# Attention projections of the second layer in scaled half-precision pairs

## The chip, the cores and the metric

The kernel runs on one core of a Trainium2 chip. The metric is the device time of one execution in microseconds (us). The core has five engines that work side by side and wait for each other through semaphores: TensorE (PE, matrix products; its weight loads are a track of their own, PEld), VectorE (DVE), ScalarE (ACT), GpSimd (POOL) and SyncE (SP). SP and POOL issue most of the DMA transfers in this kernel.

## The reference

Two layers of a backbone over 1024 latent tokens with 256 context tokens, model width 1024. The first layer mixes tokens with Fourier and Hyena channels, the second with neighbourhood attention in which the latent queries also see all context keys. Each layer ends with a SwiGLU feed-forward network (FFN). All inputs are float32. Cut to what the change touches, the second layer is:

```python
u_lat = modulate(rms_norm(h_lat, norm1_g[1]), sh1, sc1)        # (1, 1024, 1024)
u_ctx = modulate(rms_norm(h_ctx, norm1_g[1]), csh1, csc1)      # (1, 256, 1024)
q, k, v = (heads(t) for t in jnp.split(u_lat @ w_qkv, 3, axis=-1))   # 16 heads of 64
kc, vc = (heads(t) for t in jnp.split(u_ctx @ w_qkv[:, D_MODEL:], 2, axis=-1))
y_lat = neighbourhood_attention(q, k, v, kc, vc, rpb).reshape(B_, L, D_MODEL) @ w_out
h_lat = h_lat + g1 * y_lat
...
h_lat = h_lat + g2 * swiglu(modulate(rms_norm(h_lat, norm2_g[1]), sh2, sc2), ...)
```

In `neighbourhood_attention` a query of the 16 x 64 grid of latent tokens sees an 8 x 16 window of latent keys with a position bias, and all 256 context keys, under one softmax with scale 1/8.

## The kernel before

**Number format.** A product of float32 matrices is made from pairs. Each operand is split into a high part and a low remainder, and three products are added in PSUM: high x high, high x low, low x high. Two kinds of pair are in use. In the *full* kind both parts have the type `F32R`, four bytes an element (`split`, lines 287 and 289). In the *half* kind both parts are `F16` (`half_split`, lines 1153 and 1154): the operand is first multiplied by a scale, a column of per-partition numbers computed on the chip, so that it fits float16, and the result is multiplied back later. The FFNs of the latent tokens use half pairs (products at line 1342 for gate and up, at 1564 for down; some last blocks stay full). Everything else that the change touches uses full pairs, and its matmuls are issued by `mm`, line 283.

A half pair needs a bound on its operand. For weights `abs_sums` (line 1187) has ACT add up absolute values of a tile along each row, and `over_partitions` adds the rows with a small matmul. For normalised activations `operand_scale` derives the bound from the modulation columns, with a maximum over partitions on POOL (line 1172).

**Tiles.** Activations are kept transposed, in 8 blocks of 128 channels; tokens are cut into two latent pieces of 512 (`pc` 0 and 1) and the context piece of 256 (`pc` 2). A weight tile is 128 x 1024 float32, 512 KB. It is loaded into `ws`, ACT writes the high part `wh`, DVE the low part `wl`; each of the three has 2 buffers. Wide working tiles of 4 KB per partition (`S4`, name `s` in the profile) have 20 buffers, tiles of 2 KB (`S2`, also `s`) have 34. PSUM has 6 buffers `ps` and 2 `pq`.

**Stages that matter here,** in order of time:

1. First output projection (`out_proj`, about 715 to 835 us): 8 output blocks for the token pieces 2 and 0, then 8 for piece 1. Per block one weight tile, 24 matmuls of 512 columns per latent piece and 24 of 256 for the context; DVE adds the result to `h` (line 1132), ACT squares it for the next norm (line 476), POOL stores it (`ldr`, line 274).
2. FFN of the context tokens, then of the latent tokens (`ffn(0, ...)`, to about 1660 us). Near the end of gate and up, `down_scales` computes the scales of the down projection. `after2` normalises each finished piece with `norm_block` into `u1`, the input of the attention layer.
3. Values (`values`, about 1660 to 1760 us): the activations are the stationary operand, the weight halves of 512 columns are the moving one; ACT copies the result (line 1702), DVE takes its maximum (line 1703), SP stores it. After that one scale for all values is computed.
4. Attention (`attention`, about 1760 to 2260 us). `attn_prep` makes, for one pair of heads at a time, keys (three pieces) and queries (two pieces) by full-pair matmuls into `pq`; `attn_item` is a quarter of a head's queries: scores, softmax on DVE and ACT, transposes, product with the values. The loop advances three items by one step each, an older one by a later step, and after each step draws matmuls of the next pair's `attn_prep` so that these fill PE while softmax runs. `attn_out` transposes the output of a pair, multiplies it by the inverse value scale, splits it and stores both parts.
5. Second output projection: `first_part(0)`, the first 6 of 8 input blocks for piece 0, is woven into the end of the attention loop; `last_part(0)`, `first_part(1)` and `last_part(1)` follow (to about 2335 us). `add_h` (line 2141) multiplies by the modulation column and adds to `h`.

**Order.** The program is written in one order and a scheduler at compile time arranges each engine's instructions, starting what is ready and giving out tile buffers as they come free; each engine and each DMA queue then works strictly in its arranged order.

Of the kernel before, what the change touches and what calls it, by code (L numbers as in the profile page):

```python
# [19 lines left out]
P = 128  # L20
# [11 lines left out]
KSTART = (0, 8, 24, 32)  # L32
PAD_C, PAD_T, SHIFT = 120, 112, 16
BOPS = ("B11", "B21", "T2", "T1", "T3", "B22", "T4")
# [167 lines left out]
class Builder:  # L202
# [60 lines left out]

    def DR(self, shape):
        return self.dr.tile(shape, F32, name=self.nm("d"), tag=self.nm("dt"))

# [83 lines left out]
    def new_act(self, pcs=PCS, wide=True, blocks=range(KB)):  # L350

        act = Act()
        for pc in (0, 1):
            for b in blocks if pc in pcs else ():
                if wide:
                    t = self.S4(F32R)
                    act.put(0, b, pc, t[:, :512])
                    act.put(1, b, pc, t[:, 512:])
                else:
                    act.put(0, b, pc, self.S2(F32R))  # L360
                    act.put(1, b, pc, self.S2(F32R))
# [7 lines left out]
        return act  # L369

    def setup(self):
# [145 lines left out]
    def norm_block(self, x, b, pc, l, m, act, r):  # L517

        nc = self.nc
        w = WID[pc]  # L520
        sh, sc = self.ada_col(l, pc, m, b), self.ada_col(l, pc, m + 1, b)
        t = self.T()
        nc.vector.scalar_tensor_tensor(t[:, :w], x[b], sc, r[:, :w], op0=MUL, op1=MUL)
        hi, lo = act.ap(0, b, pc), act.ap(1, b, pc)
        nc.scalar.activation(hi, t[:, :w], AF.Identity, bias=sh)
        nc.vector.scalar_tensor_tensor(lo, t[:, :w], sh, hi.bitcast(F32), op0=ADD, op1=SUB)

    def norm(self, h, pcs, l, m, act):
# [584 lines left out]

    def out_proj(self, wname, y, groups, h, l, m, after):
        nc, a = self.nc, self.a
# [39 lines left out]

    def operand_scale(self, l, m):

        nc = self.nc
        conds = (0, 1) if l == 0 else (0,)
        b = self.C(4)  # L1160
        v = self.C(4)
        for c in conds:
            for k in (0, 1):
# [5 lines left out]
                                           op0=MUL, op1=ADD)  # L1169
        if l == 0:  # L1170
            nc.vector.tensor_tensor(b[:, 0:1], b[:, 0:1], b[:, 1:2], MAX)
# [8 lines left out]
        self.ucol = cols  # L1180
        self.usi = us[:, 1:2]

    def abs_sums(self, tiles, st):

        junk = self.T(BF16, 1024)
        for k, t in enumerate(tiles):
            self.nc.scalar.activation(junk[:, :t.shape[1]], t, AF.Abs, scale=2.0 ** -15, accum_out=st[:, k:k + 1])

    def over_partitions(self, sums):
# [201 lines left out]
    def ffn(self, l, u, h, hs, second, after, keep=None, begun={}):  # L1391
# [75 lines left out]
        for i in range(n2):  # L1467
# [212 lines left out]
    def values(self, u):  # L1680
# [31 lines left out]
        nc.vector.tensor_scalar(self.vs, m1, 8192.0, None, op0=MUL)  # L1712
        nc.vector.tensor_scalar(self.vsi, m2, 1.0 / 8192.0, None, op0=MUL)

    def attn_prep(self, pr, u):
# [36 lines left out]
        if pr == 0:  # L1752
            self.aw = self.weights(a["wk"][0])
# [16 lines left out]
        for pc in (0, 1):  # L1770
            for i, s in enumerate(lin(*wq, pc, acc, by_chunk)):
                if i == 3:
                    value(len(vt))
                if pc == 1 and i == 3 and pr < 7:
                    nxt = self.weights(a["wk"][pr + 1])
                yield s
            for hd in (0, 1):
                own, other = slice(hd * 64, hd * 64 + 64), slice(64 - hd * 64, 128 - hd * 64)
                qh, ql = self.S2(F32R), self.S2(F32R)
                nc.scalar.mul(qh[own], acc[pc][own], 0.125)  # L1780
                nc.vector.scalar_tensor_tensor(ql[own], acc[pc][own], 0.125, qh[own].bitcast(F32), op0=MUL, op1=SUB)
                for t in (qh, ql):
# [16 lines left out]
    def attention(self, u, fill):  # L1799
        self.prep = {}  # L1800
        self.od = [[self.DR([P, LAT]) for _ in range(2)] for _ in range(8)]
        self.banks = 6
# [127 lines left out]
    def run(self):  # L1930
# [157 lines left out]
        def after1(pcs):  # L2088
            spill(h, hs0, pcs)
            if 0 in pcs:  # L2090
# [4 lines left out]
                load_h((1,))  # L2095
                self.operand_scale(0, 3)
                for _ in self.wino_first(h, 0, 3, rs[1]):
# [11 lines left out]
        def after2(pc):  # L2109
# [15 lines left out]
        for i, _ in enumerate(self.values(u1)):  # L2125
            if i < 6:
                next(self.last, None)
        h2, o, h4 = Act(), Act(), Act()

        def load_o(b, pcs, load=None):  # L2130
            for part in (0, 1):
                if 0 in pcs:
                    t = self.S4(F32R)
                    o.put(part, b, 0, t[:, :512])
                    o.put(part, b, 1, t[:, 512:])
                for pc in pcs:
                    (load or self.ldr)(o.ap(part, b, pc).bitcast(F32), self.od[b][part][:, pc * 512:pc * 512 + 512])

        def add_h(nb, pc, acc):
            t = h2.ap(0, nb, pc)  # L2140
            nc.vector.scalar_tensor_tensor(t, acc, self.ada_col(1, pc, 2, nb), t, op0=MUL, op1=ADD)  # L2141

# [30 lines left out]
        def last_part(pc):  # L2173
            for i in (0, 1):
                wh, wl = self.weights(a["w_out2"][4 * i:4 * i + 4, :, 768:].rearrange("n p k -> p n k"), 1024, True)
                for j in range(4):
# [6 lines left out]
        for i, _ in enumerate(first_part(1)):  # L2183
            if i == 2:
                c = self.rms_begin(0)
            if i == 3:
                self.operand_scale(1, 3)
            if i == 5:
# [122 lines left out]
```

## Time and profile before

| what | value |
|---|---|
| median of 3 runs | 3006.52 us (3006.5 to 3006.53) |
| the profiled execution | 2994.77 us |
| its span, first to last instruction | 2993.0 us |
| mean granted TensorE clock | 0.984 |
| PE busy | 2844.3 us, 95%, 16366 matmuls |
| PEld busy | 1951.5 us, 65% |
| DVE / ACT / POOL busy | 71% / 55% / 18% |
| DMA | 551.49 MB, mean 184 GB/s |

How to read it: `L283 PE MATMUL ps<-s,wh 128*128 128x512 f32 x700` is a group of 700 matmuls issued at line 283, written to a PSUM tile `ps` from tiles `s` and `wh`, with a 128 x 128 stationary operand and 512 columns of four-byte elements. After the bar stand busy time in us and the mean duration of one in ns, after the next bar the idle time of the engine just before them and what ended it. Durations of neighbouring matmuls overlap in the records; the spacing of their starts is what one more of them costs a stream. A row of the table by stage gives the window, its length, busy time and instruction count of each engine, the granted clock, the DMA engines' busy share and GB/s.

### The profile page before, as it was taken

The numbers are of one execution on the slowest core, as the hardware profiler recorded it, in microseconds if no ns is written. First come the engines' busy times: TensorE is split into PE (matmuls) and PEld (weight loads), VectorE is DVE, ScalarE is ACT, GpSimd is POOL, SyncE is SP. The second block draws the span as 40 slices with busy tenths as digits, with TensorE's granted clock in tenths as the row PEclk, the third lists the DMA queues.
The fourth block names the chain that finished last, engine by engine and source line by source line (L and its number), as shares of the span: only waits on it lengthen the run. The fifth ranks groups of instructions, "written<-read, shape, count | busy, mean of one in ns | idle before, by whom it ended". The sixth has DMA issues, their size and how long they took to land. (4 is left out here: it accounts for less than half of the span.)

```text
span 2993.0 us, 46520 instructions
## 1 busy us (share of the span) xinstructions
PE 2844.3 (95%) x16366; PEld 1951.5 (65%) x16366; DVE 2132.5 (71%) x4159; ACT 1648.9 (55%) x3201; POOL 530.7 (18%) x883
## 2 busy tenths in 40 slices
PE   7899999899998999999999999999998799999997
PEld 3678888888898444444558888887786344444554
DVE  5768786684577888868876447777776888676755
ACT  4663325453456666645564337777774577564543
POOL 1012013352110111221110002222231022112000
PEclk9899999999999999999999999999999899999999
DMA  7564545357565555659864344444654376424663
GB/s 258 190 195 169 170 154 174 113 185 233 177 226 191 202 197 197 227 200 335 308 229 148 125 126 125 134 130 122 203 167 173 135 263 223 154 99 173 232 197 113
DMA packets 253684, 551.49 MB, mean 184 GB/s; under 512 B 33926, under 2 KB 69448, under 8 KB 253450
## 3 DMA queue, kind: packets, MB, share of 16 engines
q1 hardware_dynamic: 191658, 357.63, 36.5%
q0 software_dynamic: 59488, 186.70, 17.8%
q10 hardware_dynamic: 2304, 4.20, 0.4%
q8 instruction: 128, 2.10, 0.3%
q14 instruction: 106, 0.87, 0.1%
HBM read 420.20 MB, written 119.80 MB: 180 GB/s over the span
## 5 line engine op out<-in xcount | busy, mean ns | idle before, releaser
L1342 PE MATMUL ps<-s,s 128*128 128x512 f16 x2340 | 526.3, 381 | 15.4 <-ACT g L1347 12.8
L1342 PEld LDWEIGHTS <-s 128*128 128x128 f16 x2640 | 258.7, 98 | 338.6 <-issue 32.7
L283 PE MATMUL ps<-s,wh 128*128 128x256 f32 (+1 forms) x1756 | 387.9, 327 | 0.8 <-ACT wh L287 0.8
L283 PEld LDWEIGHTS ps<-s,wh 128*128 128x128 f32 x1756 | 290.0, 188 | 35.3 <-ACT wh L287 2.3
L283 PE MATMUL pq<-s,wh 128*128 128x512 f32 (+1 forms) x996 | 302.8, 383 | 4.2 <-DVE s L2141 2.9
L1564 PE MATMUL ps<-s 128*128 128x512 f16 (+2 forms) x1308 | 302.9, 378 | 2.1 <-DVE s L1154 1.7
L1153 ACT ACTIVATE s<-s,c 128x512 f16<-128x512 f32 x295 | 200.5, 715 | 118.6 <-DMA s<-d 85.7
L1564 PEld LDWEIGHTS <-s 128*128 128x128 f16 x1536 | 148.5, 98 | 179.2 <-issue 6.7
L1154 DVE SCALAR_TENSOR_TENSOR s<-s,c,s 128x512 f16<-128x512 f32 x295 | 210.5, 746 | 65.7 <-ACT s L1153 64.9
L283 PE MATMUL ps<-s,wl 128*128 128x256 f32 (+1 forms) x878 | 253.7, 327 | 2.2 <-DVE wl L289 2.2
L287 ACT CAST wh<-ws 128x1024 fp32r<-128x1024 f32 (+1 forms) x99 | 100.3, 1013 | 258.0 <-PE ps L283 173.8
L283 PE MATMUL ps<-s,s 128*128 128x64 f16 (+3 forms) x2663 | 217.6, 233 | 22.5 <-DVE st L1853 9.4
L283 PEld LDWEIGHTS pq<-s,wh 128*128 128x128 f32 x996 | 179.6, 190 | 39.3 <-DVE s L2141 3.5
L289 DVE TENSOR_TENSOR wl<-ws,wh 128x1024 fp32r<-128x1024 f32 (+1 forms) x99 | 116.5, 1177 | 118.4 <-ACT wh L287 117.2
L1342 PE MATMUL ps<-s,wh 128*128 128x512 f16 x624 | 189.9, 382 | 3.0 <-ACT wh L1153 1.7
L335 ACT CAST mat<-cs 128x1024 fp32r<-128x1024 f16 (+2 forms) x120 | 111.8, 935 | 133.6 <-PE ps L283 38.5
L283 PE MATMUL pq<-s,wl 128*128 128x512 f32 (+1 forms) x498 | 184.7, 380 | 0.5 <-DVE wl L289 0.5
L283 PE MATMUL ps<-s,mat 128*128 128x512 f32 x684 | 179.2, 409 | 5.5 <-ACT s L287 2.7
L274 POOL DMA_DIRECT2D d<-s x153 | 82.6, 541 | 518.6 <-DVE s L1410 137.1
L283 PEld LDWEIGHTS ps<-s,wl 128*128 128x128 f32 x878 | 161.3, 188 | 19.6 <-DVE wl L289 3.2
L283 PEld LDWEIGHTS ps<-s,mat 128*128 128x128 f32 x684 | 131.8, 195 | 41.3 <-DVE s L289 5.6
L283 PEld LDWEIGHTS ps<-s,s 128*128 128x128 f32 (+1 forms) x743 | 112.9, 191 | 35.2 <-DVE s L614 4.2
(410 smaller groups left out, 5734.4 us busy)
## 6 DMA issues: line engine op xcount, KB each, us to landing
s<-d SPq DMA_DIRECT2D x286, 256.0 KB, 4.4
s<-in_down SPq DMA_DIRECT2D x154, 256.0 KB, 5.1
d<-s POOLq DMA_DIRECT2D x137, 256.0 KB, 2.6
d<-tk POOLq DMA_DIRECT2D x98, 256.0 KB, 4.9
s<-in_ada_w POOLq DMA_DIRECT2D x48, 512.0 KB, 4.9
g<-in_bias POOLq DMA_DIRECT2D x128, 192.0 KB, 3.2
s<-in_up SPq DMA_DIRECT2D x46, 512.0 KB, 3.6
s<-in_gate SPq DMA_DIRECT2D x44, 512.0 KB, 4.1
```

The source lines that it names most:

```text
L274: self.last_ldr = self.nc.gpsimd.dma_start(out, in_).ins
L283: self.nc.tensor.matmul(o, l, r, start=st, stop=sp)
L287: self.last_hi = nc.scalar.copy(hi, src).ins
L289: self.last_lo = eng.tensor_tensor(lo, src, hi.bitcast(F32), SUB).ins
L335: self.nc.scalar.copy(m, st)
L1153: nc.scalar.activation(hi, src, AF.Copy, scale=scale)
L1154: nc.vector.scalar_tensor_tensor(lo, src, scale, hi, op0=MUL, op1=SUB)
L1342: nc.tensor.matmul(ps, x[:, sl], y, start=first and j == 0 and x is wh and y is xh, stop=j == 3 and x is wl, skip_group_check=True)
L1564: m = nc.tensor.matmul(acc[j][:, c0:c1], x[:, sl], y[:, xs], start=first and k == 0, stop=last and k == 2, skip_group_check=True)
```

## The change

- **Weights.** A new `weights16` loads a tile as before and makes a half pair with a scale. It replaces `weights` for the tiles of `wv`, `wk`, `wq` and `w_out2`.
- **Activations.** `norm_half` writes `u1` as half pairs, from modulation columns that are multiplied by the scale; `new_half` gives two blocks of a latent piece one wide tile, where one block had one.
- **Scales.** `qkv_sums` loads all 32 tiles of the four weights on POOL's queue into wide tiles and has ACT take their absolute sums. It is a generator that is drawn on once per output block of the first output projection, two tiles each. `qkv_scales` turns the sums into four weight scales and the inverse factors, near the end of the FFN of the first layer.
- **Undoing the scales.** The inverse factors are folded into multiplications that stood there already: the queries' 0.125 becomes the column `qinv`; the inverse value scale takes up `oinv` and goes into a scaled modulation column `g2col`, used by `add_h`.
- **Attention output.** `attn_out` writes both parts into one `F16` tile and stores them in one transfer; `load_o` reads them back the same way.
- Some small column tiles are added, and a padding tile grows from 120 to 136 numbers per partition.

The diff, cut to its core:

```diff
+    def weights16(self, src, scale, w=1024, cut=False, load=None):
+        st = self.pw.tile([P, 1024], F32, tag="ws", name=self.nm("ws"))
+        hi, lo = (self.pw.tile([P, 1024], F16, tag=g, name=self.nm(g)) for g in ("wh", "wl"))
+        (load or self.ld)(st.rearrange("p (n k) -> p n k", n=4) if cut else st[:, :w], src)
+        self.half_split(st[:, :w], scale, hi[:, :w], lo[:, :w])
+        return hi, lo
...
+    def norm_half(self, x, b, pc, act, r, cols):
...
+        nc.vector.scalar_tensor_tensor(t[:, :w], x, sc, r[:, :w], op0=MUL, op1=MUL)
+        hi, lo = act.ap(0, b, pc), act.ap(1, b, pc)
+        nc.scalar.activation(hi, t[:, :w], AF.Identity, bias=sh)
+        nc.vector.scalar_tensor_tensor(lo, t[:, :w], sh, hi, op0=ADD, op1=SUB)
...
                 acc = self.lin(wh, wl, 0, range(KB), y, pcs)
+                next(fill, None)
...
+    def qkv_sums(self):
+        a = self.a
+        self.qs = self.C(32)
+        src = [a["wv"][ch, kp] for ch in range(2) for kp in range(4)]
+        src += [a[n][b] for n in ("wq", "wk", "w_out2") for b in range(KB)]
+        for k, x in enumerate(src):
+            t = self.S4()
+            self.ldr(t, x)
+            self.abs_sums([t], self.qs[:, k:k + 1])
+            if k % 2:
+                yield
...
+    def qkv_scales(self):
+        nc = self.nc
+        bounds = self.over_partitions(self.qs.rearrange("p (i k) -> p i k", k=1))
+        t = self.C(8)
+        nc.vector.tensor_reduce(t[:, :4], bounds.rearrange("p (i k) -> p i k", k=8), axis=AX, op=MAX)
...
+        self.u1col, usi = self.operand_scale(1, 0, (0, 1))
...
                 scales = self.down_scales(l, nh)
+                if l == 0:
+                    self.qkv_scales()
...
-                    wh, wl = self.weights(a["wv"][ch, kp])
+                    wh, wl = self.weights16(a["wv"][ch, kp], self.wscale["wv"])
...
-                    wq = self.weights(a["wq"][pr])
+                    wq = self.weights16(a["wq"][pr], self.wscale["wq"])
...
-                nc.scalar.mul(qh[own], acc[pc][own], 0.125)
+                nc.scalar.mul(qh[own], acc[pc][own], self.qinv[own])
...
-        oh, ol = self.TK(F32R), self.TK(F32R)
-        nc.scalar.mul(oh, ps, self.vsi)
-        nc.vector.scalar_tensor_tensor(ol, ps, self.vsi, oh.bitcast(F32), op0=MUL, op1=SUB)
-
-        self.ldr(self.od[pr][0][:, hf * 512:hf * 512 + 512], oh.bitcast(F32))
-        self.ldr(self.od[pr][1][:, hf * 512:hf * 512 + 512], ol.bitcast(F32))
+        t = self.TK(F16, 1024)
+        nc.scalar.copy(t[:, :512], ps)
+        nc.vector.tensor_tensor(t[:, 512:], ps, t[:, :512], SUB)
+        self.ldr(self.od[pr][hf], t)
...
-        self.out_proj("w_out", y, [(2, 0), (1,)], h, 0, 2, after1)
+        self.out_proj("w_out", y, [(2, 0), (1,)], h, 0, 2, after1, self.qkv_sums())
...
-                    u1.t.update(self.new_act(pcs=(pc,), blocks=(b, b + 1)).t)
-                self.norm_block({b: h3.ap(0, b, pc)}, b, pc, 1, 0, u1, r)
+                    self.new_half(u1, pc, b)
+                self.norm_half(h3.ap(0, b, pc), b, pc, u1, r, self.u1col)
...
-                wh, wl = self.weights(a["w_out2"][nb, :, :768], 768, load=None if pc else self.ldr)
+                wh, wl = self.weights16(a["w_out2"][nb, :, :768], self.wscale["w_out2"], 768, load=None if pc else self.ldr)
```

More of the change, by code (lines that the diff above doesn't have):

```diff
@@ L262, in C, with DR @@
         return self.cp.tile([p, w], dt, name=self.nm("c"), tag=self.nm("ct"))
-    def DR(self, shape):
-        return self.dr.tile(shape, F32, name=self.nm("d"), tag=self.nm("dt"))
+    def DR(self, shape, dt=F32):
+        return self.dr.tile(shape, dt, name=self.nm("d"), tag=self.nm("dt"))
     def ld(self, out, in_):
@@ L369, in new_act, with new_half @@
         return act
+    def new_half(self, act, pc, b):
+        w = WID[pc]
+        t = self.S4(F16, 2048) if pc < 2 else self.S2(F16, 1024)
+        for k in range(4):
+            act.put(k % 2, b + k // 2, pc, t[:, k * w:(k + 1) * w])
+    def weights16(self, src, scale, w=1024, cut=False, load=None):
[4 more added lines that the diff above has]
+        return hi, lo
     def setup(self):
@@ L1111, in fourier_c, with out_proj @@
             self.split(raws[g][:, :256], y.ap(0, g, 2), y.ap(1, g, 2))
-    def out_proj(self, wname, y, groups, h, l, m, after):
+    def out_proj(self, wname, y, groups, h, l, m, after, fill):
         nc, a = self.nc, self.a
@@ L1712, in values @@
         nc.vector.tensor_scalar(self.vs, m1, 8192.0, None, op0=MUL)
-        nc.vector.tensor_scalar(self.vsi, m2, 1.0 / 8192.0, None, op0=MUL)
+        nc.vector.tensor_scalar(self.vsi, m2, 1.0 / 8192.0, self.oinv, op0=MUL, op1=MUL)
+        self.g2col = self.C(8)
+        nc.vector.tensor_scalar(self.g2col, self.ada[(1, 0)][:, 16:24], self.vsi, None, op0=MUL)
     def attn_prep(self, pr, u):
@@ L1752, in attn_prep @@
         if pr == 0:
-            self.aw = self.weights(a["wk"][0])
+            self.aw = self.weights16(a["wk"][0], self.wscale["wk"])
         acc = {}
@@ L1774, in attn_prep @@
                 if pc == 1 and i == 3 and pr < 7:
-                    nxt = self.weights(a["wk"][pr + 1])
+                    nxt = self.weights16(a["wk"][pr + 1], self.wscale["wk"])
                 yield s
@@ L1800, in attention @@
         self.prep = {}
-        self.od = [[self.DR([P, LAT]) for _ in range(2)] for _ in range(8)]
+        self.od = [[self.DR([P, LAT], F16) for _ in range(2)] for _ in range(8)]
         self.banks = 6
@@ L2128, in run @@
         h2, o, h4 = Act(), Act(), Act()
+        ot = {}
         def load_o(b, pcs, load=None):
[L2131 to L2137, printed above, removed]
+            if 0 in pcs:
+                ot[b] = self.S4(F16, 2048)
+            for pc in pcs:
+                t = ot[b][:, pc * 1024:pc * 1024 + 1024]
+                (load or self.ldr)(t, self.od[b][pc])
+                for part in (0, 1):
+                    o.put(part, b, pc, t[:, part * 512:part * 512 + 512])
         def add_h(nb, pc, acc):
             t = h2.ap(0, nb, pc)
-            nc.vector.scalar_tensor_tensor(t, acc, self.ada_col(1, pc, 2, nb), t, op0=MUL, op1=ADD)
+            nc.vector.scalar_tensor_tensor(t, acc, self.g2col[:, nb:nb + 1], t, op0=MUL, op1=ADD)
         def load_h2(nb, pc):
@@ L2174, in last_part @@
             for i in (0, 1):
-                wh, wl = self.weights(a["w_out2"][4 * i:4 * i + 4, :, 768:].rearrange("n p k -> p n k"), 1024, True)
+                wh, wl = self.weights16(a["w_out2"][4 * i:4 * i + 4, :, 768:].rearrange("n p k -> p n k"),
+                                        self.wscale["w_out2"], 1024, True)
                 for j in range(4):
```

29 lines of the change are left out of this document (20 added, 9 removed).

## The prediction

> **What bounds the kernel now.** I read the page's busy times and slices first, then the table by stage, then the rows by line and the timeline of the stages that change.
>
> ```profile
> span 2993.0 us, 46520 instructions
> PE 2844.3 (95%) x16366; PEld 1951.5 (65%) x16366; DVE 2132.5 (71%) x4159; ACT 1648.9 (55%) x3201; POOL 530.7 (18%) x883
> PE   7899999899998999999999999999998799999997
> ...
> 715.00:835.00 120.00, 120.00 (x635) 102.38 (x633) 65.33 (x101) 45.98 (x72) 12.99 (x24) 1.00 0.51 184
> ...
> 1660.00:1762.00 102.00, 102.00 (x444) 83.02 (x443) 38.06 (x56) 30.12 (x44) 1.38 (x1) 1.00 0.37 125
> 1762.00:2260.00 498.00, 466.60 (x4204) 399.33 (x4204) 358.62 (x934) 350.09 (x989) 129.41 (x241) 0.99 0.49 146
> 2260.00:2335.00 75.00, 67.70 (x292) 50.34 (x291) 56.00 (x83) 35.08 (x60) 14.51 (x27) 0.93 0.54 195
> ```
>
> TensorE is busy nearly everywhere. The four stage rows (columns: window, length, then busy time with instruction count of PE, weight loads, DVE, ACT, POOL, then clock, DMA share, GB/s) are the first output projection, the values, attention with queries and keys woven in, and the tail of the second output projection. In the first two PE never stops; in attention it idles 31.4 us, in the tail 7.3. So a matmul that takes fewer nanoseconds shortens the run directly in the values, mostly in attention, partly in the tail.
>
> Durations of single matmuls overlap, so their price is the spacing of starts. I take it from windows and stretches that hold one kind only.
>
> ```profile
> 1670.00:1710.00 40.00, 40.00 (x174) 1.00 0.35 117
> 1150.00:1240.00 90.00, 90.00 (x418) 1.00 0.64 212
> 860.00:900.00 40.00, 40.00 (x354) 1.00 0.53 177
> 1766.61 0.48 PE L283 MATMUL pq<-s,wh 128*128 128x256 f32 x2
> 1769.54 0.65 PE L283 MATMUL pq<-s,wh 128*128 128x512 f32 x2
> 1781.14 0.76 PE L283 MATMUL ps<-s,s 128*128 128x256 f32 x4
> 1781.74 0.63 PE L283 MATMUL pq<-s,wh 128*128 128x512 f32 x2
> 1787.23 1.94 PE L283 MATMUL ps<-s,s 128*128 128x256 f32 x12
> 2289.07 0.63 PE L283 MATMUL ps<-s,wh 128*128 128x512 f32 x2
> 2294.66 0.63 PE L283 MATMUL ps<-s,wh 128*128 128x512 f32 x2
> ```
>
> Row 1, values, line 283 alone: 40.00/174 = 229.9 ns per 512 columns. Row 2, the half-precision products of line 1342: 90.00/418 = 215.3 ns. Row 3, line 283 in the context FFN, 256 columns: 113.0 ns. The timeline rows bound stretches whose counts the loops give: keys of the context, 24 matmuls of 256 columns from 1766.61 to 1769.54, 122.1 ns; queries, 48 from 1769.54 to 1781.14, 241.7 ns; keys, 24 from 1781.74 to 1787.23, 228.8 ns; second output projection, 24 from 2289.07 to 2294.66, 232.9 ns. Queries and output projection read their moving operand in runs of 16 elements, the keys in one run: the stride costs full precision 4 to 13 ns.
>
> **The change part by part.** *Matmuls.* Their number stays, three products per pair; each gets half-precision operands.
>
> Values: 10 token blocks x 2 halves x 8 x 3 = 480, times (229.9 - 215.3) = 7.0 us, all kept since PE never waits there.
>
> Keys of the latent: 8 head pairs x 48 = 384, times (228.8 - 215.3) = 5.2 us. Queries: 384, times (241.7 - 215.3) = 10.1 us if the stride costs half precision nothing, 5.2 if the 12.9 ns stay; no row shows a strided half-precision operand of this width, I take the middle, 7.7. Keys of the context: 192; half of 215.3 is the floor, so 2.8 us at most, 0 at least; by the nearest row, 113.0, it is 1.7. Second output projection: 2 x 8 x 8 x 3 = 384, times 17.6 = 6.8 us, or 1.8 with 12.9 ns of stride left; the middle is 4.3. Of these 384, 144 run inside attention (1.6 us), 240 after it (2.7 us).
>
> Gross: 7.0 + 5.2 + 7.7 + 1.7 + 4.3 = 25.9 us, between 19.2 and 31.9.
>
> *What attention keeps.* 5.2 + 7.7 + 1.7 + 1.6 = 16.2 us fall there, as matmuls that fill the time in which an item's softmax runs.
>
> ```profile
> 2007.90:2066.70 58.80, 54.61 (x513) 46.88 (x513) 43.54 (x116) 42.95 (x124) 15.12 (x29) 1.00 0.45 128
> PE ps L283 <- DVE st L1853: 9.4, 10, 1.5
> PE ps L1865 <- DVE s L1869: 5.0, 9, 0.7
> PE ps L1865 <- DVE st L1853: 3.4, 4, 1.0
> ```
>
> A head pair takes 58.8 us with 54.6 of PE; DVE and ACT have 15 us to spare, so no other engine's throughput takes over. But the waits (rows 2 to 4, of attention alone) are for softmax steps: where the filler shrinks just ahead of such a wait, the wait grows. The start of the softmax moves forward too, since its scores come from the same, faster stream. I keep 60%: 9.7 us, between 0 and 16.2.
>
> *The tail.* In the two last parts 6 matmuls (6 x 232.9 = 1.40 us) make one block, whose update and square cost DVE as much:
>
> ```profile
> L481 DVE TENSOR_TENSOR tk<-tk,tk 128x512 f32<-128x512 f32 x52 | 35.6, 684 | 1.9 <-ACT tk L476 0.8
> L2141 DVE SCALAR_TENSOR_TENSOR s<-ps,c,s 128x512 f32<-128x512 f32 x17 | 12.7, 747 | 5.7 <-PE ps L283 5.6
> ```
>
> 684 + 747 = 1.43 us: there 96 of the 240 gain nothing. 144 keep 144/240 x 2.7 = 1.6 us.
>
> *Splits.* A weight tile's split becomes a scaled copy and a fused subtract (rows: line, engine, operation, count, then busy us, mean ns, then idle before):
>
> ```profile
> L287 ACT CAST wh<-ws 128x1024 fp32r<-128x1024 f32 x83 | 87.0, 1049 | 240.3 <-PE ps L283 163.7 <-PE pq L283 32.9 <-issue 21.2
> L1153 ACT ACTIVATE wh<-ws,c 128x1024 f16<-128x1024 f32 x44 | 50.5, 1147 | 23.3 <-DVE c L1210 11.5 <-PE pq L1342 5.4 <-PE ps L1342 5.0
> L289 DVE TENSOR_TENSOR wl<-ws,wh 128x1024 fp32r<-128x1024 f32 x83 | 101.3, 1221 | 118.0 <-ACT wh L287 116.8 <-PE ps L283 0.6
> L1154 DVE SCALAR_TENSOR_TENSOR wl<-ws,c,wh 128x1024 f16<-128x1024 f32 x44 | 56.3, 1280 | 25.8 <-ACT wh L1153 25.8
> ```
>
> 98 ns more on ACT and 59 on DVE per tile. In the values a tile feeds 24 or 36 matmuls, over 5 us; ACT is busy 30 of 102 us. Nothing; uncovered it would be 0.16 us a tile, 52 tiles, 8 us. The norm that makes the activations keeps its three instructions, the attention output loses 61 ns of DVE and one of two stores. The activations take 8 wide buffers of 20 instead of 16, which can only let transfers start earlier; no row puts a TensorE wait on those buffers, so I take 0, at most the 6.3 us that PE idles in this stretch at the end of the first FFN:
>
> ```profile
> 1565.00:1610.00 45.00, 38.66 (x279) 33.93 (x278) 38.60 (x58) 28.08 (x45) 4.23 (x8) 1.00 0.45 154
> ```
>
> *Weight sums.* 32 loads of 512 KB on POOL's queue and 32 absolute sums on ACT enter the first output projection, two per column block.
>
> ```profile
> 720.00:745.00 25.00, 25.00 (x145) 21.84 (x144) 8.99 (x14) 5.92 (x9) 3.28 (x6) 1.00 0.27 95
> 770.00:795.00 25.00, 25.00 (x135) 21.36 (x134) 8.74 (x14) 8.72 (x16) 2.16 (x4) 1.00 0.44 144
> 815.00:835.00 20.00, 20.00 (x106) 17.07 (x104) 18.67 (x25) 11.57 (x15) 2.16 (x4) 1.00 1.02 406
> L1187 ACT ACTIVATE t<-ws 128x1024 bf16<-128x1024 f32 x43 | 45.0, 1047 | 4.5 <-DVE s L1154 3.3 <-DMA ws<-in_gate 0.8 <-DMA ws<-in_up 0.4
> L1187 ACT ACTIVATION_READ_ACCUMULATOR t<-ws x43: 185/187/200, 954.3 to 2692.5; 128x1 f32 x43
> L274 POOL DMA_DIRECT2D s<-in_ada_w x48 | 25.8, 539 | 173.6 <-DVE c L450 71.7 <-DVE s L1154 42.3 <-DMA s<-d 16.1
> ```
>
> ACT: 32 x (1.047 + 0.187) = 39.5 us, beside 46.0 of 120. Transfers: 16.8 MB over 120 us is 140 GB/s beside 184; the last 20 us are full already (406 GB/s, prefetch of the next stage's weights), the first 75 nearly empty. POOL: 32 x 0.539 = 17 us beside 13.0; queued behind are the stores of h, which TensorE doesn't wait for. Ahead of TensorE only the 16 weight casts on ACT (1.05 us each) matter: one has most of a block (PE needs 24 x 0.230 + 24 x 0.122 = 8.4 us for a block of the first group, 24 x 0.230 = 5.5 in the second) to spare. I take 0.
>
> *Scales.* One reduction, one small matmul, an all-reduce on POOL, some column arithmetic near the end of the first FFN, on sums finished 500 us before. The nearest small matmul chain cost PE 8.4 us where it followed its sums at once (first row below), the all-reduce 0.376 us; behind it on POOL wait stores that nobody needs for tens of us. I take 0.5, up to 8.4.
>
> ```profile
> PE ps L283 <- DVE st L1195: 8.5, 2, 8.4
> L1172 POOL PARTITION_ALL_REDUCE c<-c x2: 375/376/377, 413.6 to 1460.4; - x2
> ```
>
> Net: 7.0 + 9.7 + 1.6 - 0.5 = 17.8 us. The profiled execution took 2994.8 us (span 2993.0), the median of the runs is 3006.5, 11.7 more; the same saving gives 2977 and **2988.7 us**. About 0.2% of it, 6 us, is what a measurement can tell from no change.
>
> **The rivals.** *Attention takes its share back.* Every wait on the softmax grows by what its filler lost. For: all large PE waits there are of that kind. Against: 15 us of DVE and ACT free per head pair. Then 7.0 + 1.6 - 0.5 = 8.1 are left: 2998.4.
>
> *Short runs are slow in half precision.* Runs of 16 elements are now 32 bytes; if they cost twice full precision's 12.9 ns, queries take 241.1 ns and gain nothing, the output projection loses 384 x 8.2 = 3.1 us. Left are 7.0 + 0.6 x 6.9 - 3.1 - 0.5 = 7.5: 2999. No row speaks for or against. In this case the change doesn't do what it says for the half of it.
>
> *The sums hold up the casts (slower).* ACT works in order. If a block's two loads are issued only at their place, ACT stands until they land, and the next cast behind them. Landing is slower from POOL's queue:
>
> ```profile
> s<-in_ada_w POOLq DMA_DIRECT2D x48, 512.0 KB, 4.9
> s<-in_up SPq DMA_DIRECT2D x46, 512.0 KB, 3.6
> L476 ACT ACTIVATE tk<-s 128x512 f32<-128x512 f32 x60 | 37.2, 628 | 33.8 <-DVE s L1585 15.1 <-DVE s L1132 7.4 <-DVE s L2141 6.1
> ```
>
> ACT's round, with the cast and a square of h, is then 4.9 + 0.5 + 2 x 1.23 + 1.05 + 0.63 = 9.6 us against 8.4 in eight blocks and 5.5 in eight: 8 x 1.2 + 8 x 4.1 = 42 us, so 3006.5 - 17.8 + 42 = 3031. It decides from 17.8/16 = 1.1 us lost per block. Against it: of 20 wide buffers the projection's input holds 8, so loads can run several blocks ahead; and the sums over fresh loads that stand in the FFN now (line 1187) had ACT wait for a DMA 0.8 + 0.4 us in 43 of them. The Trainium skill (SBUF — State Buffer, the "DVE blocks DMA" trap under its two separate sides) says that descriptors of a POOL-issued DMA wait while VectorE holds the shared port; it would make those landings later when DVE is busy. The row of 4.9 us against 3.6 goes that way, but names no cause.
>
> **How the numbers follow.** Forecast 0.62 (2975 to 2995); attention takes its share back 0.20, two thirds of it under 3000.5; short runs slow 0.08, likewise; sums hold up the casts 0.10. Faster: 0.62 + 0.13 + 0.05 = 0.80; same: 0.07 + 0.03 = 0.10; slower 0.10. The low end is the whole upper gross plus a little of the buffers, 3006.5 - 33.5 = 2973; the high end, 3007, takes in both milder rivals and leaves out the slower one.
>
> **What would show it.** Right: about 216 ns per matmul in the values, which end 7 us shorter; weight loads of 98 instead of 188 ns; queries under 230 ns; attention some 10 us shorter, with PE's idle time there up from 31 to 38 us; PE without gaps from 715 to 835 although ACT there is near 85 us. Wrong: gaps of PE on the weight split in that stretch, or an attention of 498 us with more idle.

## The result, and the profile after

The changed kernel takes 2977.2 us (median of 4 runs, 2972.24 to 2980.3) beside 3006.51 us of the kernel before on the same chip; the ratio is 0.9907, 95% interval 0.9885 to 0.9929. A second comparison, on the chip of its variants, gave 0.9912 (0.9896 to 0.9927). The profiled execution took 2972.24 us, 22.5 less than the profiled one of before, which had been 11.7 us under its own median. By the medians the gain is 29.3 us; the account below is of profiled executions.

The head of the page after, and the table by stage (the windows are set by the same instructions as before, so they have moved; columns as in the prediction; 835 to 900 us is the start of the context FFN):

```profile
span 2970.4 us, 46594 instructions
PE 2817.3 (95%) x16367; PEld 1808.1 (61%) x16367; DVE 2138.6 (72%) x4178; ACT 1689.6 (57%) x3265; POOL 537.8 (18%) x896
```

```profile
715.00:835.00 120.00, 120.00 (x623) 101.94 (x622) 64.58 (x107) 63.15 (x109) 25.66 (x48) 1.00 0.63 230
835.00:900.00 65.00, 52.34 (x373) 48.96 (x372) 37.09 (x49) 41.56 (x65) 7.77 (x16) 0.84 0.82 323
1690.00:1784.00 94.00, 93.86 (x436) 42.69 (x435) 38.27 (x56) 30.46 (x44) 0.35 (x1) 1.00 0.40 134
1784.00:2253.00 469.00, 448.03 (x4240) 317.49 (x4239) 366.04 (x939) 353.81 (x993) 121.65 (x226) 1.00 0.47 141
2253.00:2321.00 68.00, 58.11 (x257) 26.42 (x256) 52.28 (x78) 34.56 (x58) 11.86 (x22) 0.90 0.55 193
```

The values stage is 8 us shorter, attention 29, the tail 7; together more than the whole gain, so something was lost elsewhere. It shows in the second row: the first output projection has no gap, but of the 65 us after it PE idles 12.7. The same row of the kernel before has 1.4:

```profile
835.00:900.00 65.00, 63.59 (x547) 62.90 (x546) 50.02 (x66) 35.64 (x53) 5.93 (x11) 1.00 0.55 189
```

To see where time goes and comes from, the start of each instruction that both traces have was set against its start before. The table (worked out from the traces, medians of 40 us from the time named; columns: time in the kernel before, then us later or, with a minus, earlier) shows two executions of the changed kernel and two variants told of below:

```
from us       after  after_again  sums_only  early
 680 first output projection
               4.9       0.9         7.2       4.9
 880 context FFN
              25.0      19.0        23.8       6.9
1200          23.4      20.4        23.9       4.7
1280          27.3      25.9        24.6      10.3
1640 values begin
              29.1      26.4        23.7       9.5
1760 attention begins
              21.2      18.9        23.6       1.4
2240 attention ends
              -7.4      -6.5        15.9     -23.2
2320 tail ends
             -14.1     -14.0        15.7     -33.6
2560 second FFN
             -24.3     -23.2        11.5     -46.5
```

What stands at 680 us lies ahead of the change's first instruction and differs between executions by some us. From there the two executions of the changed kernel agree: 18 to 20 us lost at the start of the context FFN, 4 to 6 lost around 1250 us, where the new scales are computed, then 7.5 to 7.9 won in the values, 25 to 29 in attention, 7 in the tail, 9 to 10 in the second FFN.

**The products.** Line 283 alone in the values; then, from the timeline, where the context's keys begin, where the queries begin, and a later query; then a weight load of the values after and (from the trace before) before:

```profile
1700.00:1740.00 40.00, 39.85 (x186) 1.00 0.36 119
```

```profile
1789.30 0.39 PE L283 MATMUL pq<-s,wh 128*128 128x256 f16 x2 [1.10 <-DVE s L1826]
1791.93 0.59 PE L283 MATMUL pq<-s,wh 128*128 128x512 f16 x2
1798.40 0.59 PE L283 MATMUL pq<-s,wh 128*128 128x512 f16 x2
```

```profile
L283 PEld LDWEIGHTS <-s 128*128 128x128 f16 x402 | 39.3, 98 | 47.6 <-issue 0.4
```

```profile
L283 PEld LDWEIGHTS ps<-wh,s 128*128 128x128 f32 x202 | 37.9, 188 | 8.5
```

40.00/186 = 215.1 ns in the values. Context keys, 24 from 1789.30 to 1791.93: 109.6 ns (122.1 before). Queries, 30 from 1791.93 to 1798.40: 215.7 ns, as fast as operands that lie in one run; before they took 241.7. So runs of 16 elements cost half precision nothing, and the queries' term belongs at its upper end. The Trainium skill (TensorE: Matmul & The Clock Gate, "Wait — 56ns, not 53.3ns?") gives 215.7 ns from start to start at 512 columns and full clock; the queries show that number.

**The loss at 840 us.** Waits of PE, and two of ACT's, in 835 to 900 us of the changed kernel; then its clock; then, from the timeline of POOL and SP and SP's waits, when the late sum loads and the first gate weight are issued, and how long transfers issued in 833 to 850 us take to land:

```profile
PE ps L283 <- ACT wh L287: 5.1, 2, 4.9
PE pq L283 <- ACT t L519: 4.3, 1, 4.3
PE pq L283 <- DVE tk L495: 2.3, 1, 2.3
ACT s L1292 <- DVE s L1305: 5.0, 2, 2.9
ACT t L1212 <- DMA s<-in_w_out: 4.7, 4, 1.4
```

```profile
835.00:860.00 25.00, 22.05 (x148) 20.74 (x147) 10.12 (x12) 18.64 (x30) 4.31 (x9) 0.86 1.03 419
860.00:880.00 20.00, 10.28 (x52) 8.22 (x51) 10.43 (x15) 11.69 (x22) 1.61 (x3) 0.66 0.91 355
880.00:900.00 20.00, 20.00 (x178) 20.00 (x178) 16.55 (x22) 11.23 (x15) 1.85 (x4) 1.00 0.48 169
```

```profile
825.61 4.20 POOL L274 DMA_DIRECT2D s<-in_wk  x8
833.43 2.17 POOL L274 DMA_DIRECT2D s<-in_w_out  x4 [3.62 <-PE ps L283]
833.32 0.33 SPq L268 DMA_DIRECT2D s<-in_gate  x1
SPq L268 <- DMA s<-in_wk: 11.3, 1, 11.3
```

```profile
s<-in_w_out POOLq DMA_DIRECT2D x8, 512.0 KB, 18.6
s<-in_gate SPq DMA_DIRECT2D x5, 512.0 KB, 11.3
```

The first 16 sum loads stand at the start of the projection, where DMA was free. The other 16 are drawn in the second group of output blocks, and in the arranged order they come out only from 825.6 us on, at the end of it. There they share 419 GB/s with the next stage's gate and up weights, which in the kernel before began to load at:

```profile
813.40 0.38 SPq L268 DMA_DIRECT2D s<-in_gate  x1
```

The first gate weight is now issued 20 us later: both kinds of load fill wide tiles, and SP's queue stands 11.3 us until a sum's load of `wk` has landed. From 833 to 850 us transfers take 11 to 19 us to land, ACT stands four times for a sum's load with the norm (line 519) and a cast (line 287) queued behind it, and PE waits for both. The gaps also pull the granted clock to 0.66; it is 1.00 again from 880 us on. The Trainium skill (TensorE: Matmul & The Clock Gate, "What's actually happening") has the clock at half after an idle window of about 3.4 us until as long a busy one; two waits of 4.9 and 4.3 us with a low mean around them fit that.

### The profile page after: what moved, and what is told of

It reads as the page before. It is cut to its first block, busy times and chain, and to the rows that moved or that the text cites. A ratio compares the mean times of both kernels' runs of the same rounds, so it can differ in the third digit from the quotient of the medians.

```text
span 2970.4 us, 46594 instructions
## 1 busy us (share of the span) xinstructions
PE 2817.3 (95%) x16367; PEld 1808.1 (61%) x16367; DVE 2138.6 (72%) x4178; ACT 1689.6 (57%) x3265; POOL 537.8 (18%) x896
## 4 chain that ended last, share of the span: by engine, by line
PE 41%; issue 20%; DVE 7%; DMA 5%; ACT 3%; POOL 3%; SPq 0%; POOLq 0%; DVEq 0%; ACTq 0%
PE ps L1396 11%; PE ps L283 10%; PE pq L283 7%; PE ps L1620 5%; PE pq L1396 3%; POOL d L274 2%; PE ps L1723 2%; PE ps L1923 2%; PE pq L1620 1%; DMA s<-in_w_out 1%; DMA s<-d 1%; DMA cs<-in_vi_l 1%; DVE s L1181 1%; ACT t L1212 0%; DMA g<-in_bias 0%
## 5 line engine op out<-in xcount | busy, mean ns | idle before, releaser
L1396 PE MATMUL ps<-s,s 128*128 128x512 f16 x2304 | 515.5, 380 | 4.4 <-ACT tk L1401 4.4
L1396 PEld LDWEIGHTS <-s 128*128 128x128 f16 x2640 | 257.6, 98 | 318.7 <-issue 10.8
L283 PE MATMUL ps<-s,wh 128*128 128x256 f32 (+2 forms) x1768 | 394.5, 329 | 6.1 <-ACT wh L287 5.7
L283 PEld LDWEIGHTS ps<-s,wh 128*128 128x128 f32 x1648 | 273.5, 191 | 35.4 <-ACT wh L287 8.4
L283 PE MATMUL pq<-s,wh 128*128 128x512 f16 (+3 forms) x984 | 279.4, 365 | 3.5 <-DVE s L1826 2.2
L283 PE MATMUL ps<-s,wl 128*128 128x256 f32 (+2 forms) x884 | 257.8, 329 | 4.6 <-DVE wl L1181 3.7
L1620 PEld LDWEIGHTS <-s 128*128 128x128 f16 x1536 | 148.4, 98 | 178.9 <-issue 6.7
L1181 DVE SCALAR_TENSOR_TENSOR wl<-ws,c,wh 128x1024 f16<-128x1024 f32 (+1 forms) x96 | 118.7, 1237 | 88.2 <-ACT wh L1180 88.1
L1180 ACT ACTIVATE wh<-ws,c 128x1024 f16<-128x1024 f32 (+1 forms) x96 | 106.7, 1112 | 123.9 <-PE ps L283 43.7
L283 PE MATMUL pq<-s,wl 128*128 128x512 f16 (+3 forms) x492 | 174.9, 365 | 0.0
L283 PEld LDWEIGHTS <-s 128*128 128x128 f16 x2400 | 111.9, 98 | 63.5 <-issue 2.5
L283 PEld LDWEIGHTS <-wh 128*128 128x128 f16 x896 | 86.1, 98 | 90.2 <-issue 9.1
```

The lines of the kernel that those rows point to most:

```text
L283: self.nc.tensor.matmul(o, l, r, start=st, stop=sp)
L1180: nc.scalar.activation(hi, src, AF.Copy, scale=scale)
L1181: nc.vector.scalar_tensor_tensor(lo, src, scale, hi, op0=MUL, op1=SUB)
L1396: nc.tensor.matmul(ps, x[:, sl], y, start=first and j == 0 and x is wh and y is xh, stop=j == 3 and x is wl, skip_group_check=True)
L1620: m = nc.tensor.matmul(acc[j][:, c0:c1], x[:, sl], y[:, xs], start=first and k == 0, stop=last and k == 2, skip_group_check=True)
```

## The experiments

**Without the sums.** `qkv_sums` shrinks to one memset of `qs`.

```diff
-        for k, x in enumerate(src):
-            ...
+        self.nc.vector.memset(self.qs, 1.0 / 16.0)
+        yield
```

> The changed kernel without the thirty-two weight sums: the scales of values, keys, queries and output projection come from a constant in place of the sum, everything else stands. Theory (the sums are not free: their second half is loaded on top of the gate and up weights of the context FFN and holds the casts up): the 17.7 us that the changed kernel's trace had lost by the start of the context FFN are not lost, so about 2977 - 17 = 2960 us, PE idle in 835 to 900 us back from 12.7 to a few us, DMA under 0.5 there outside the first 10 us of the prefetch. Rival (that delay is chance of the run or of the order written for the engines, and the sums are free as predicted): 2977 us, within 3. Attention stays at 469 us by both.

Measured: 2950.45 us beside 2998.13 (ratio 0.9841, 0.9826 to 0.9855), against 0.9907 and 0.9912 with the sums: 0.7%, 20 us. The start of the context FFN has its old row back (below). The sums were not free.

**The sums earlier.** Four tiles per draw, so all 32 belong to the first eight output blocks.

```diff
-            if k % 2:
+            if k % 4 == 3:
```

> The changed kernel with four blocks of sums drawn per step in place of two, so that all thirty-two loads and sums are asked for beside the first group of output blocks and none beside the second. Theory (it is the late half, loaded from 825 us on, that collides with the gate and up weights): the second half moves to 760 to 825 us, where the changed kernel's DMA share was 0.37 to 0.45 and ScalarE nearly idle; about 2960 us, and the context FFN's weights land from 813 us on again. Rival A (any sum costs its ScalarE time wherever it is put): 2977 us. Rival B (more loads at once hold up the casts of the output projection itself, 715 to 745 us at 1.02 of the DMA): 2985 us or more, with gaps of PE on L287 before 835 us.

Measured: 2949.2 us, ratio 0.9835 (0.9819 to 0.9852). The same sums, all of them done, cost nothing against leaving them out. That refutes rival A, and B too: PE keeps its 120 us although DMA now runs at 0.81. The rows of 715 to 835 and 835 to 900 us, of the early sums, and the second row without sums and with sums only:

```profile
715.00:835.00 120.00, 120.00 (x621) 101.93 (x620) 61.22 (x99) 75.92 (x134) 29.01 (x55) 1.00 0.81 311
835.00:900.00 65.00, 62.85 (x521) 61.59 (x521) 52.69 (x70) 36.30 (x52) 5.96 (x11) 0.97 0.58 213
```

```profile
835.00:900.00 65.00, 63.58 (x541) 62.59 (x540) 50.51 (x66) 35.29 (x51) 5.96 (x11) 1.00 0.58 212
```

```profile
835.00:900.00 65.00, 52.86 (x388) 50.16 (x387) 39.24 (x53) 42.34 (x68) 8.95 (x17) 0.87 0.84 328
```

**Sums alone in the kernel before.** `qkv_sums` is drawn by `out_proj` as in the change, its result unused; the padding tile grows to 216 numbers.

> The kernel before with the thirty-two loads and sums added during the first output projection as the change has them, their results not used; all second-layer weights and activations stay in full-width pairs. Theory: 3006.5 + 17 = 3023 us, with the start of the context FFN late by 12 to 18 us. Rival (sums free): 3006.5 us within 3.

Measured: 3005.66 us beside 2998.13, ratio 1.0024 (1.0013 to 1.0035). The row above has the loss of the changed kernel, and the table of starts shows it: 7.2 to 23.8, 16.6 us. But 8 us come back at the end of attention and 4 in the second FFN, so the whole is 7 us slower and not 17. In the change the two stages run another way, and the loss stays.

**The second output projection in full pairs.** Weights, attention output and `add_h` as before, the rest as changed.

```diff
-        t = self.TK(F16, 1024)
-        nc.scalar.copy(t[:, :512], ps)
-        nc.vector.tensor_tensor(t[:, 512:], ps, t[:, :512], SUB)
-        self.ldr(self.od[pr][hf], t)
+        oh, ol = self.TK(F32R), self.TK(F32R)
+        ...
-                wh, wl = self.weights16(a["w_out2"][nb, :, :768], self.wscale["w_out2"], 768, load=None if pc else self.ldr)
+                wh, wl = self.weights(a["w_out2"][nb, :, :768], 768, load=None if pc else self.ldr)
```

> The changed kernel with the second output projection back in full-width pairs (its weights, the attention's output and its scale as before); values, keys and queries stay in half-precision pairs, the sums stay. By the spacing of the rows the projection's 384 products of 512 columns go from 216 to about 233 ns, 6.5 us, of which 7 of 24 steps lie in the attention. Theory (the attention's stalls went for reasons of the key and query products): attention 469 to 472 us, the whole 2977 + 7 = 2984 us, tail 5 to 7 us longer. Rival (the smaller attention output and its fewer and smaller stores took the stalls away): attention 480 us or more, the whole 2993 us or more. Third: nothing outside the tail's buffers, 2979 us.

Measured: 2999.57 us beside 2998.13, ratio 1.0003 (0.9991 to 1.0015): all of the gain is gone. From the first scores to the last value product attention is 25 us longer than in the changed kernel (473.4 against 448.3; the 469 us of the expectation are a wider window), though the projection has only 144 of its 384 products in it, at its end. The first head pair is as long as in the change, the others are longer. Neither number of the theory held; the rival's did, but its reason had yet to be found. The order in which PE's instructions are arranged differs: between the 8 items of a head pair, the change in full has one item with no matmul of the next pair ahead of it, this variant two, as the kernel before. Three kernels try that.

**Sixteen wide tiles again, all in half precision.**

```diff
-        t = self.S4(F16, 2048) if pc < 2 else self.S2(F16, 1024)
-        for k in range(4):
-            act.put(k % 2, b + k // 2, pc, t[:, k * w:(k + 1) * w])
+        for j in range(2):
+            t = self.S4(F16, 2048) if pc < 2 else self.S2(F16, 1024)
+            for k in range(2):
+                act.put(k, b + j, pc, t[:, k * w:(k + 1) * w])
```

> The changed kernel in which each half-precision pair of the second layer's normed activations gets a wide tile for two blocks in place of four, so that sixteen wide tiles are held through the attention as in the kernel before, in place of eight; every product stays in half precision. In the order in which the kernel issues its products, the 8 items of a head pair then have the fillers of before between them: 0, 4.5, 0.6, 5.1, 0, 5.1, 5.0, 2.8 us (two items with none) against 0, 4.5, 0.6, 5.1, 4.3, 2.2, 5.2, 1.3 in the changed kernel (worked out from the order of the instructions and the 214 ns of a filler product). Theory (the stalls beyond the products' saving went because the fillers came to lie more evenly, not because of half precision as such): attention from first scores to last value product 465 to 475 us, against 448 in the changed kernel and 473 with the output projection in full, idle of PE near 35 us against 20; the whole 2977 + 20 = 2997 us. Rival (shorter products and weight loads alone took the stalls away): 448 us and 2977 us.

Measured: 2980.91 us beside 3000.81, ratio 0.9929 (0.9909 to 0.9948). Attention takes 457.5 us with 29.0 idle: 9 us of the 33 that the change had won there are lost (6 beside the second execution of the change, which took 451.4), between the two theories.

**Pacing 5.5 in the kernel before.** Full pairs throughout.

```diff
-                while done < (k * 3 + stage + 5) * n / 24:
+                while done < (k * 3 + stage + 5.5) * n / 24:
```

> The kernel before with one number changed: the constant 5 that sets how far the next head pair's projections run ahead of the softmax steps becomes 5.5. All products stay full-width pairs. In its issue order every second head pair then has the fillers 0, 5.0, 0.7, 5.7, 4.8, 1.0, 6.8, 1.9 us between its items (as the changed kernel's order), the others 0, 4.8, 1.0, 5.7, 0, 5.7, 3.0, 5.7 (as before). Theory (order): pairs of the first kind lose 2 to 3 us of stalls each, four of them 8 to 12 us, so attention 470 us against 481.6 and the whole 2996 us. Rival (half precision): 3006.5 us.

Measured: 2991.04 us, ratio 0.9969 (0.9956 to 0.9982); attention 471.4 us against 481.6. This is the clearest of the three, since one execution holds both orders, in turn, at one precision: head pairs of 55.4 us with 1.6 idle and of 58.2 with 3.8 (rows below).

**Pacing 4 with the early sums.** Constant 4 in place of 5.

> The changed kernel with all sums beside the first group of output blocks, and the constant 5 of the pacing replaced by 4. Its issue order has three of eight items of a head pair without filler (0, 0, 6.4, 3.9, 0, 6.1, 1.6, 5.1 us). Theory (order): stalls as before or worse, attention 470 to 480 us against 448 to 452, the whole some 20 to 30 us over the same kernel with 5 (ratio to before 0.990 to 0.994 against 0.9835). Rival (half precision took the stalls away): attention 450 us, ratio 0.9835.

Measured: ratio 0.9841 (0.9819 to 0.9862) against 0.9835. Attention took 457.6 us with 26.2 idle, 6 us more than with constant 5, far less than expected.

**Another buffer for the attention's output, with the early sums.**

```diff
-        t = self.TK(F16, 1024)
+        t = self.S2(F16, 1024)
```

> The changed kernel with all sums beside the first group of output blocks and one buffer moved: the tile that takes the attention's output before it is stored comes from the pool of narrow tiles in place of the pool of four. All products stay in half precision, no work is added. Its issue order has two items without filler per head pair again: 0, 4.5, 0.6, 5.1, 0, 7.4, 2.7, 2.8 us. Theory (order): a steady head pair takes 55 to 56 us with 3 to 4 us of idle as with sixteen wide tiles, against 53.4 and 1.4; attention 460 us; some 12 us over the same kernel with the tile left where it is. Rival (half precision took the stalls away, wide tiles were a matter of their own): 53.4 us a pair, no difference.

Measured: ratio 0.9834 (0.981 to 0.9857), no difference. Its steady head pairs take 54 to 55 us and idle 2.3 to 2.7, about 1 more than the change's, between theory and rival, and the end of its attention is shorter by about as much. Of the four forecasts made by counting items without filler, the one for pacing 5.5 held, sixteen wide tiles came halfway, and these last two missed. The count says too little; whether it matters where such items stand was not tried.

Steady head pairs, one or two of each kernel, from the first value product of one to that of the next (length, PE busy first). Before; pacing 5.5 in full pairs; the change; sixteen wide tiles; other buffer; pacing 4; projection in full:

```profile
1978.55:2037.31 58.76, 54.59 (x514) 46.86 (x512) 43.50 (x116) 42.92 (x123) 15.08 (x28) 1.00 0.45 129
```

```profile
1926.30:1981.72 55.42, 53.87 (x512) 46.46 (x512) 42.60 (x113) 41.32 (x122) 14.55 (x28) 1.00 0.47 135
1981.72:2039.97 58.25, 54.50 (x514) 46.37 (x512) 44.74 (x119) 43.65 (x126) 15.65 (x30) 1.00 0.43 130
```

```profile
1989.32:2042.87 53.55, 52.18 (x514) 37.92 (x513) 43.83 (x116) 43.12 (x124) 14.04 (x26) 1.00 0.44 131
```

```profile
1994.06:2050.00 55.94, 52.93 (x514) 37.83 (x512) 44.69 (x118) 43.61 (x126) 14.30 (x27) 1.00 0.42 126
```

```profile
2022.55:2077.12 54.57, 52.01 (x512) 37.75 (x512) 44.52 (x117) 43.54 (x125) 14.65 (x28) 1.00 0.43 127
```

```profile
1965.85:2022.21 56.36, 52.60 (x512) 37.61 (x512) 44.18 (x116) 43.41 (x126) 14.54 (x27) 1.00 0.43 130
```

```profile
1994.85:2053.16 58.31, 53.10 (x513) 38.69 (x512) 43.93 (x116) 43.28 (x123) 15.14 (x28) 0.97 0.44 131
```

Read length minus PE busy as idle: 4.2; 1.6 and 3.8; 1.4; 3.0; 2.6; 3.8; 5.2 us. PE busy goes with the number format: 53.9 to 54.6 us in full pairs, 52.0 to 53.1 in half. Idle does not: both formats have long and short ones.

The same over the whole attention, from the first scores to the last value product, before, the change, and the projection in full:

```profile
1781.25:2262.85 481.60, 450.30 (x4138) 385.86 (x4137) 352.36 (x924) 342.22 (x976) 128.38 (x239) 0.99 0.49 147
```

```profile
1802.41:2250.74 448.33, 428.46 (x4138) 307.48 (x4137) 354.70 (x923) 344.12 (x976) 118.70 (x221) 1.00 0.46 140
```

```profile
1798.85:2272.28 473.43, 435.06 (x4138) 323.96 (x4137) 355.85 (x924) 344.69 (x976) 128.88 (x239) 0.99 0.49 150
```

33.3 us are won: 21.8 of PE busy, 11.4 of idle. With the projection in full, 15.2 of busy are won and 7.1 of idle come on top.

**The change and the early sums side by side.**

> The changed kernel itself, on the chip of its variants: 0.989 to 0.993 of before, to set the variants beside it.

> The changed kernel with all sums beside the first group of output blocks, on the same chip as the changed kernel: theory 15 to 21 us below it (ratio to before 0.982 to 0.986); if the two medians lie within 6 us, what was read as a collision was a difference of chips or runs.

Measured on one chip: 2974.25 us (ratio 0.9912) and 2946.68 us (0.9818, 0.9801 to 0.9834), beside 3000.96. The difference is 27.6 us by the medians, more than expected, and 18.6 by the two profiled executions, of which the early one was the slowest of its four. The change with early sums beats both kernels. Of its lead over the change 14 to 18 us arise at 840 us by the starts; the tail gives 2 to 4 more (10 won there instead of 7), for which no experiment was made.

## Why the prediction was right

The forecast, 2988.7 in 2973 to 3007, is 11.5 us above the median; the sign was right, and so was the main mechanism, that cheaper products shorten the stages TensorE fills. That the sum came near is luck: sums and scales cost some 23 us more than forecast, attention, tail and second FFN gave some 31 more.

- *Values*, 7.0: 480 x (229.9 - 215.1) = 7.1 us by the products; 7.5 to 7.9 by the starts. Right, and nothing waits there.
- *Queries and output projection*, middle of two ends: the upper end holds. 384 x (241.7 - 215.7) = 10.0 us for the queries instead of 7.7. The rival of slow short runs is refuted by the 215.7 ns.
- *What attention keeps*, 9.7 of 16.2: the step that failed most, with 25 to 29 us by the starts. Gross was too low: PE busy in attention fell by 18.3 to 21.8 us in two executions of the changed kernel, since the stride costs nothing (the upper end of the terms was 5.2 + 10.1 + 2.8 + 6.8 x 144/384 = 20.7). And the waits on softmax did not grow from 31 to 38 us; they fell to 20. The mechanism behind the 60% is not refuted: with the projection in full, idle is 38.4 us and attention 8.2 us shorter than before, close to the 38 and 9.7 forecast; but that is another kernel in another order, and no test of it. What the step left out is that the arranged order of PE changes with formats and buffers. Shown: order alone moves a head pair by 2.8 us at one precision. Not shown: what in the change leads to the better order, and why idle is longest with the projection in full.
- *The tail*, 1.6: about 7. At the upper end the 240 products there give 4.2; the wait of before in the next fence, for a block's square, is also gone after. That DVE would hold two fifths of the gain back was wrong; with the projection in full the tail gains nothing (10.4 to 10.9 us in the starts), so it is the projection's own.

```profile
PE pq L283 <- DVE tk L481: 3.9, 1, 3.9
```

- *Weight sums*, 0: 17 to 20 us lost by the starts. The prediction looked at the right engines, and saw the full DMA of the last 20 us. But it took two loads per block as spread over the stage. ACT shows it: 63 us there instead of the 85 forecast, since half of the sums ran later. The slower rival had the mechanism, ACT standing at a sum whose load is late with a cast behind it, but at every block; it came at one place, where loads of the next stage wanted the same tiles and queues; with the sums drawn earlier it did not come at all.
- *Scales*, 0.5, up to 8.4: the term was mis-sized, 4 to 6 us. They are computed around 1265 us of the changed kernel, and there the starts fall back: by 3.9 and 5.5 us in its two executions (1200 to 1280 in the table), 5.6 with the early sums, 5.9 without sums, but 0.7 with sums alone. So it goes with the scales and not with the sums; no run leaves out the scales alone. In the first three rows (of the changed kernel) DVE stands for the all-reduce on POOL, which itself takes 0.38 us, and the steps behind it on DVE, which free PE's tiles, come late; PE waits 5.5 us in 1200 to 1310 us, where it waited 1.8 before (row 4). The prediction looked at what waits behind the all-reduce on POOL, and not at DVE, which waits for its result; the trace before had it for the two all-reduces there (row 5).

```profile
DVE c L1200 <- POOL c L1198: 4.1, 1, 4.1
PE ps L1396 <- ACT tk L1401: 4.2, 2, 3.5
PE ps L1396 <- DVE g L1410: 1.3, 1, 1.3
PE ps L1342 <- ACT g L1347: 1.8, 1, 1.8
DVE c L1174 <- POOL c L1172: 8.7, 2, 5.2
```

- *Left out:* 9 to 10 us won in the second FFN. There PE of the kernel before idles in 2420 to 2600 us, waiting for ACT, and ACT for a store that must free its tile; the change has no such gap:

```profile
PE ps L1342 <- ACT g L1347: 10.4, 3, 5.4
ACT g L1347 <- DMA d<-g: 11.2, 3, 4.1
```

```profile
2420.00:2600.00 180.00, 169.36 (x772) 75.75 (x771) 140.55 (x246) 122.61 (x245) 40.96 (x76) 0.97 0.60 218
```

```profile
2420.00:2600.00 180.00, 180.00 (x845) 81.64 (x844) 142.65 (x248) 122.65 (x239) 37.28 (x69) 1.00 0.55 200
```

With sums alone, 4 us of it were won, with the projection in full about 11, so it does not need a cheaper output projection. Whether it hangs on the time at which the stage is entered, or which edit sets it, was not tried.

So for the second execution of the changed kernel, forecast against starts: sums 0 and -18, scales -0.5 and -5.5, the rest up to the values 0 and -2, values 7.0 and 7.5, attention 9.7 and 25, tail 1.6 and 7.5, second FFN 0 and 9: 17.8 and 24, less 0.9 from ahead of the change.

## What to carry to other kernels

Work put "once per block" into a stage runs where the arranged order lets its loads start, so look for the next stage's prefetch at that stage's end and draw extra loads before it; here that was one line and 0.7 to 0.9%. In a stage that weaves filler matmuls between dependent steps, price the busy time by the spacing of starts, and treat the idle time as a property of the arranged order, which edits of formats and buffers reshuffled here: order alone moved a head pair by 2.8 us, the cheaper products took 2.4 off its busy time. Price a short instruction by what waits for its result, on every engine, not by its duration: the scales, with an all-reduce of 0.38 us, cost 4 to 6. Before crediting a gain to arithmetic, look for one execution that holds both orders at the same precision.

## What the hardware showed that was not expected

- A moving operand in runs of 16 elements costs full-width products 4 to 13 ns of 512 columns, and half-precision ones nothing: 215.7 ns against 215.1. Over the whole attention, the median spacing of neighbouring full-width products was 227 ns for keys (one run), 240 for queries and 235 for the output projection (runs of 16), and 216 for each of the three in the change. The run length is not all that sets it: context keys, in one run, had 120 ns at 256 columns beside the 113.0 of the context FFN.
- While the next stage's weights are fetched, a 512 KB load takes far longer to land than the 3.6 us (SP) and 4.9 us (POOL) of the prediction's rows: SP's gate weights took 7.7 us in the kernel before (812 to 835 us, 375 GB/s), 10.6 with the early sums (815 to 850, 365 GB/s), both without a sum's load beside them, and 11.3 in the change (833 to 850, 419 GB/s), where POOL's took 18.6. So late landing alone is not what cost the 18 to 20 us.
